# RG-LRU gates in quarters of TensorE, with the convolution's result and a half-swapped copy of it

## The chip, the cores and the metric

The kernel runs on one core of one Trainium2 chip. The metric is device time in microseconds (us) of one execution. The kernel before took 1862.1 us (median of 3 runs, 1861.45 to 1863.89).

## The reference

A two-layer trunk (D_MODEL 1024, 256 context tokens and 256 latent tokens). Each layer normalises, projects, runs three token mixers side by side, merges them, projects again, and ends with a squared-ReLU MLP. The change is inside the first mixer, the RG-LRU:

```
def rglru_coeffs(xc, a_w, a_b, x_w, x_b, lam):
    xh = xc.reshape(bn, n, LRU_BLOCKS, LRU_BLOCK_W)           # 16 blocks of 64 channels
    r = sigmoid(einsum('bnhi,hij->bnhj', xh, a_w) + a_b)      # gate r
    i = sigmoid(einsum('bnhi,hij->bnhj', xh, x_w) + x_b)      # gate i
    log_a = -8 * r * softplus(-lam)
    a = exp(log_a)
    u = sqrt(-expm1(2 * log_a)) * (i * xc)
    return a, u                                # then a linear scan h = a * h + u over the tokens
```

`xc` is a depthwise convolution (4 taps) of the projection `lx`; both directions of the scan have gate weights of their own. The output is the sum of the two directions' scans times `gelu(ly)`, where `ly` is another projection. So for each block of 64 channels four 64x64 matrices multiply the same `xc`: two gates, two directions.

## The kernel before

Activations lie with channels on the 128 partitions and the 512 tokens (context, then latent) along the free axis. A 1024x1024-type product is split in output slices of 128 channels. Each slice is one `gemm` (L216): the weight tile is loaded by SyncE's (SP's) DMA queue (`wraw`), split by ScalarE (ACT) into a rounded part `wh` (L200) and by VectorE (DVE) into the rest `wl` (L201), and then 24 matmuls of 128x512 on TensorE (PE) add up in one PSUM bank of the pool `mm` (4 banks). Three raw tiles and three split tiles are in flight, so the split of a slice waits for the product three slices earlier. Other PSUM work uses the 4 banks of the pool `mx`.

The RG-LRU stage of a layer handles 8 slices of 128 channels (two blocks each), i = 0 to 7:

- `lru_conv(i)`: a gemm of slice i of `lx` (below: **conv i**), then ACT L552 and three DVE operations L555 make `xc` of slice i.
- `lru_gates(i)` (**gate call i**): the block-diagonal 128x128 weights of slice i (`gw`, two blocks with zeros beside them) multiply `xc` in plain fp32, once for each direction and gate, four matmuls of 128x512 (L566), each into an `mx` bank. ACT empties each bank with a Tanh (L567), makes another Tanh for each direction (L571), and DVE multiplies by `xc` (L572).
- `lru_decay(i)`: two Exp on ACT (L578). For each pair of slices one Sqrt follows (L710), and then `lru_scan` of both on DVE (L585 to L595), whose result `yh` ACT rounds (L307).
- `gate_y(j)` (**branch gate j**): a gemm of slice j of `ly`, emptied by Gelu on ACT (L544). It is 128x512 in layer 0 and half as wide in layer 1, the last.

Exp, Gelu and Sqrt each need a table of functions that ACT loads (ACT_TABLE_LOAD) when it goes from one to another; Tanh is in the tables of Gelu and Exp, not in that of Sqrt. The order of the stage before, in layer 0, behind conv 0 and 1 and branch gates 0 to 2: gate call 0, conv 2, gate call 1, branch gates 3 and 4, conv 3, gate call 2, conv 4, gate call 3, branch gates 5 and 6, a small product for the next mixer, conv 5, gate call 4, conv 6, gate call 5, branch gate 7, conv 7, two gemms of the next mixer (GLA: its k and q), gate calls 6 and 7. The next mixer's first head (`gla`, its scores are the matmuls of L793) follows.

A tile scheduler orders each engine's instructions when the program is built, from program order, priorities (`tc.high_priority`) and its own estimates; on the chip each engine takes its list strictly in that order, and an instruction that waits holds back all that stand behind it.

Of the kernel before, what the change touches and what calls it, by code (L numbers as in the profile page):

```python
# [15 lines left out]
F32 = mybir.dt.float32  # L16
# [26 lines left out]
NL = 2  # L43
# [61 lines left out]
def trunk_kernel(ctx: ExitStack, tc: tile.TileContext, out: bass.AP, d: dict):  # L105
    nc = tc.nc
    V, S, G, P = nc.vector, nc.scalar, nc.gpsimd, nc.tensor
# [11 lines left out]
    sm = ctx.enter_context(tc.tile_pool(name="sm", bufs=2))  # L119
# [3 lines left out]
    def tmp():  # L123
        return t2.tile([128, 512], F32, name="t2")
# [16 lines left out]
    def mx():  # L141
        return ps_mx.tile([128, 512], F32, name="mx")
# [61 lines left out]
    def weight(*key, hi=None, lo=None, ahead=AHEAD):  # L204
        with tc.high_priority(ahead):
            return weight_parts(weight_raw(*key), hi, lo)
# [308 lines left out]
    for l in range(NL):  # L515
# [22 lines left out]
        def gate_y(i):  # L538
            if l == 0 and i < 3:
                ps = first_ps[i]  # L540
            else:
                ps = gemm(weight(l, "in", O_LY + 128 * i, hi=E_LYH), hh, hl, c0)
            ge[i] = x[:, i, :256] if last else tmp()
            S.activation(ge[i], ps, AF.Gelu_apprx_tanh)  # L544

        xcs = {}

        def lru_conv(i):
            ps = gemm(weight(l, "in", O_LX + 128 * i, hi=E_LXH, lo=E_LXL, ahead=AHEAD if l or i > 1 else 0), hh, hl, 0)
            xc = xcs[i] = tmp()  # L550

            S.activation(xc, ps, AF.Identity, scale=pc(l, "cw", 8 + i, 1), bias=pc(l, "cb", i, 1))  # L552
            x3, p3 = (a.rearrange("p (s t) -> p s t", s=2) for a in (xc, ps))
            for k, (a, b) in ((0, (1, 256)), (2, (0, 255)), (3, (0, 254))):
                V.scalar_tensor_tensor(x3[:, :, a:b], p3[:, :, a + k - 1:b + k - 1], pc(l, "cw", 8 * k + i, 1),  # L555
                                       x3[:, :, a:b], op0=ALU.mult, op1=ALU.add)

        def lru_gates(i):
            xc = xcs.pop(i)
            gw = sm.tile([128, 4, 128], F32, name="gw")  # L560
            nc.sync.dma_start(gw, d["lruw"][l, i])
            rt, tt, ix = (t[:, i % 4] for t in ws_)
            for dd in range(2):
                for q, dst in ((0, rt), (1, ix)):
                    pg = mx()
                    P.matmul(pg, gw[:, 2 * dd + q, :], xc, start=True, stop=True)  # L566
                    S.activation(dst[:, dd, :], pg, AF.Tanh, scale=0.5,  # L567
                                 bias=habx[:, l, 16 * q + 8 * dd + i:16 * q + 8 * dd + i + 1])

                c2p = c2[:, l, 1, 8 * dd + i:8 * dd + i + 1]  # L570
                S.activation(tt[:, dd, :], rt[:, dd, :], AF.Tanh, scale=c2p, bias=c2p)  # L571
                V.scalar_tensor_tensor(ix[:, dd, :], ix[:, dd, :], 1.0, xc, op0=ALU.add, op1=ALU.mult)  # L572
# [117 lines left out]
        LYS = LYS0, LYS1  # L690
        ly = iter(range(8))
# [4 lines left out]
            gate_consts()  # L696
        for i in range(0, 8, 2):
            lru_conv(i + 1)
            if i < 6:
                lru_gates(i)  # L700
                lru_conv(i + 2)
            else:

                kq0 = gla_kq(0)
                lru_gates(i)
            lru_gates(i + 1)
            for j in range(2):
                lru_decay(i + j)
            tt = ws_[1][:, i % 4:i % 4 + 2]
            S.activation(tt, tt, AF.Sqrt, scale=0.25, bias=epsc)  # L710
            for j in range(LYS[l][i // 2 + 1]):
                gate_y(next(ly))
            if i == 6:
                gates0 = gla_gates(0)
                v0 = gla_v(0)
            for j in range(2):
                lru_scan(i + j)
            if i == 6:
                ys0 = gla_r(0)
            if i == GZP:  # L720
                zs = gla_z()
# [367 lines left out]
        for c in range(5):  # L1089
            if c < 4:  # L1090
                hid[c] = ytiles(("yh", "yl")[c % 2])
                n = NSPL if c == 0 and not last else 0
# [28 lines left out]
def layout(inp):  # L1121

    import numpy as np

    f = np.float32
    A = {k: np.asarray(v) for k, v in inp.items()}
    a = {}

    def ktile(w, c, n):
        return w[:, c:c + n].reshape(8, 128, n).transpose(1, 0, 2)  # L1130

    tiles = []
    for l in range(NL):
        for w in weight_order(l):
            if w[0] == "in":
                tiles.append(ktile(A["w_in"][l], w[1], 128))
            elif w[0] == "tok":
                tiles.append(ktile(A["w_in"][l], w[1], 512)[:, 2 * w[2]:2 * w[2] + 2])
            elif w[0] == "br":
                tiles.append(ktile(A["w_branch"][l, w[1]], 128 * w[2], 128))  # L1140
            elif w[0] == "out":
                tiles.append(ktile(A["w_out"][l], 128 * w[1], 128))
            elif w[0] == "w1":
                tiles.append(ktile(A["mlp_w1"][l], 128 * w[1], 128))
            else:
                tiles.append(ktile(A["mlp_w2"][l][1024 * w[1]:1024 * w[1] + 1024], 128 * w[2], 128))
    a["wt"] = np.stack([t.reshape(128, 1024) for t in tiles])
    mw = A["mod_w"].reshape(NL, 8, 128, 12, 512)
    mw = mw[:, :, :, [0, 2, 1, 3] + list(range(4, 12))]
    mw = mw.reshape(NL, 8, 128, 6, 2, 512).transpose(0, 3, 4, 2, 1, 5).copy()  # L1150
    m0 = mw[0, :2].reshape(2, 2, 128, 8, 2, 256)
    mw[0, :2] = m0.transpose(0, 4, 2, 3, 1, 5).reshape(2, 2, 128, 8, 512)
    a["mod_w"] = mw
    xt = np.concatenate([A["ctx"][0], A["x"][0]], axis=0).T
    a["xt"] = np.ascontiguousarray(xt.reshape(8, 128, T).transpose(1, 0, 2))
    a["cs"] = np.stack([A["c_ctx"].reshape(8, 128).T, A["c"][0].reshape(8, 128).T], axis=2)
    par = np.zeros((128, NL, NPAR), f)

    def put(l, name, v):
        lo, hi = PCOLS[name]  # L1160
        par[:, l, lo:hi] = v.reshape(hi - lo, 128).T

    for l in range(NL):
        put(l, "n1", A["norm1_g"][l])
        put(l, "n2", A["norm2_g"][l])
        put(l, "modb", A["mod_b"][l])
        put(l, "cw", A["conv_w"][l])
        put(l, "cb", A["conv_b"][l])
        put(l, "ab", A["lru_a_b"][l])
        put(l, "xb", A["lru_x_b"][l])  # L1170
        put(l, "lam", A["lru_lambda"][l])
        put(l, "gb", A["gla_gate_b"][l])
        put(l, "gng", A["gla_norm_g"][l])
        put(l, "qg", A["q_norm_g"][l])
        put(l, "kg", A["k_norm_g"][l])
    a["par"] = par
    lruw = np.zeros((NL, 8, 128, 4, 128), f)
    for dd in range(2):
        for q, name in enumerate(("lru_a_w", "lru_x_w")):
            w = A[name][:, dd].reshape(NL, 8, 2, 64, 64)  # L1180
            for s in range(2):
                lruw[:, :, 64 * s:64 * s + 64, 2 * dd + q, 64 * s:64 * s + 64] = w[:, :, s]
    a["lruw"] = lruw
    glaw = np.zeros((NL, 3, 32, 2, 512), f)
    for dd in range(2):
        glaw[:, :, 16 * dd:16 * dd + 16, dd] = A["gla_gate_w"][:, None, dd]
    glaw = glaw.reshape(NL, 96, 2, 512)
    a["glaw"] = glaw
    a["wz"] = np.stack([ktile(A["w_in"][l], O_GZ, 32) for l in range(NL)])
    dim = np.arange(128)  # L1190
    swap = dim ^ 32
    rg = np.stack([A["q_norm_g"], A["q_norm_g"][:, swap], A["k_norm_g"], A["k_norm_g"][:, swap]], axis=1)
    a["ropeg"] = np.ascontiguousarray(np.broadcast_to(rg[:, None], (NL, 128, 4, 128)))
    t = np.arange(256)
    inv = (f(10000.0) ** (-np.arange(0, 64, 2, dtype=f) / f(64))).astype(f)
    ang = np.where(dim[None] < 64, (t // 64).astype(f)[:, None], (t % 64).astype(f)[:, None]) * inv[dim % 32][None]
    ang = ang.astype(f)
    sgn = np.where(dim % 64 < 32, f(-1), f(1))
    rc = np.stack([np.cos(ang), np.sin(ang) * sgn[None]]).astype(f)
    a["ropec"] = np.ascontiguousarray(rc.reshape(2, 2, 128, 128).transpose(2, 0, 1, 3))  # L1200
    a["ident"] = np.eye(128, dtype=f)
    j = np.arange(128)
    a["masks"] = np.stack([(j[:, None] <= j[None]).astype(f), (j[:, None] >= j[None]).astype(f)], axis=1)
    a["rmask"] = np.ascontiguousarray(np.broadcast_to((np.arange(T) % 64 != 0).astype(f), (128, T)))
    return {k: np.ascontiguousarray(v) for k, v in a.items()}
# [16 lines left out]
```

## Time and profile before

| | |
|---|---|
| median of 3 runs | 1862.1 us (1861.45 to 1863.89) |
| the profiled execution | 1860.73 us, span 1858.9 us, mean granted TensorE clock 0.993 |
| PE matmul busy | 1803.0 us (97%) |
| DVE busy | 1288.0 us (69%) |
| ACT busy | 936.3 us (50%) |
| gate matmuls (L566) | 128 records, 60.0 us |
| gate weights by DMA | 16 loads of 256.0 KB |

The gate matmuls appear as 128 records because one fp32 matmul is recorded as two. A record's duration includes pipeline time that overlaps its neighbours; what a matmul costs a dense stream is the distance between starts. PE is near fully busy over the whole span, but the shares of DVE and ACT differ from stage to stage: in the RG-LRU stages of both layers ACT is much busier than its 50%.

### The profile page before, as it was taken

The page shows a single profiled execution, that of the slowest core. Times are in us where ns is not written, and L with a number is a line of the kernel's source. Part 1 is how long each engine was busy: PE and PEld are TensorE (multiplying, and loading weights), DVE is VectorE, ACT ScalarE, POOL GpSimd, SP SyncE. Part 2 cuts the span into 40 slices and gives each one's busy share as a digit, 9 for nine tenths or more (in the row PEclk, how much of TensorE's full clock was granted, in tenths as well). Part 3 has the DMA queues.
Part 4 walks back from the last instruction along what each step waited for, and adds up shares of the span by engine and source line. Part 5 has one row for each costly group of instructions (what it writes and reads, how often), then busy time and mean ns, then how long its engine had stood idle before and what let it go on. Part 6 is the DMA issues. An engine that isn't in the chain of part 4 may idle for free.

```text
span 1858.9 us, 26345 instructions
## 1 busy us (share of the span) xinstructions
PE 1803.0 (97%) x9992; PEld 1496.2 (80%) x9992; DVE 1288.0 (69%) x2206; ACT 936.3 (50%) x1620; POOL 62.8 (3%) x87
## 2 busy tenths in 40 slices
PE   5999999999999999999999999999999999999999
PEld 4766788888787888988888889767889877878887
DVE  4786775454557777789763447797876588778776
ACT  4787545333444333564332325788665455556443
POOL 1000000000000000000000000000000000000000
PEclk9999999999999999999999999999999999999999
DMA  8322222232211556666753235522333432755554
GB/s 324 102 76 85 70 82 80 70 102 80 68 57 52 196 188 201 215 219 208 237 178 100 91 95 184 173 92 85 109 101 122 131 125 91 261 170 159 186 188 148
DMA packets 82143, 255.59 MB, mean 137 GB/s; under 512 B 9184, under 2 KB 12384, under 8 KB 81248
## 3 DMA queue, kind: packets, MB, share of 16 engines
q1 hardware_dynamic: 82016, 253.90, 42.0%
q8 instruction: 79, 1.29, 0.3%
q14 instruction: 48, 0.39, 0.1%
HBM read 252.82 MB, written 1.05 MB: 137 GB/s over the span
## 4 chain that ended last, share of the span: by engine, by line
PE 59%; issue 22%; DVE 9%; ACT 7%; POOL 1%; DMA 1%; SPq 0%; POOLq 0%; DVEq 0%; ACTq 0%
PE mm L216 48%; PE mx L216 5%; DVE wl L201 2%; PE mx L841 2%; ACT lru L567 1%; PE mx L220 1%; PE mx L822 1%; ACT wh L200 1%; ACT lru L710 1%; DVE lru L586 1%; PE mx L566 1%; DVE lru L588 1%; ACT lru L571 1%; PE mx L793 1%; DMA wraw<-wt 1%
## 5 line engine op out<-in xcount | busy, mean ns | idle before, releaser
L216 PE MATMUL mm<-h,wh 128*128 128x512 f32 (+1 forms) x2512 | 729.6, 370 | 7.1 <-ACT h L307 5.1
L200 ACT CAST wh<-wraw 128x1024 fp32r<-128x1024 f32 x365 | 382.2, 1049 | 500.9 <-PE mm L216 391.5
L201 DVE TENSOR_TENSOR wl<-wraw,wh 128x1024 fp32r<-128x1024 f32 x365 | 445.5, 1222 | 235.6 <-ACT wh L200 219.9
L216 PEld LDWEIGHTS mm<-h,wh 128*128 128x128 f32 x2512 | 452.4, 189 | 91.5 <-issue 7.2
L216 PE MATMUL mm<-h,wl 128*128 128x512 f32 (+1 forms) x1448 | 493.9, 341 | 0.0
L216 PEld LDWEIGHTS mm<-h,wl 128*128 128x128 f32 x1448 | 274.0, 189 | 31.6 <-issue 1.4
L216 PE MATMUL mm<-yh,wh 128*128 128x512 f32 (+1 forms) x640 | 224.7, 351 | 2.2 <-DVE big L1039 2.1
L216 PE MATMUL mm<-yh,wl 128*128 128x512 f32 (+1 forms) x640 | 224.0, 350 | 0.0
L216 PE MATMUL mm<-yl,wh 128*128 128x512 f32 (+1 forms) x640 | 222.4, 348 | 0.0
L216 PE MATMUL mm<-yp,wh 128*128 128x512 f32 (+1 forms) x576 | 183.6, 374 | 2.5 <-ACT g L873 2.3
L216 PE MATMUL mm<-wh,h 128*128 128x512 f32 x576 | 183.4, 395 | 0.0
L216 PE MATMUL mm<-yp,wl 128*128 128x256 f32 x512 | 145.1, 283 | 0.0
L370 DVE SCALAR_TENSOR_TENSOR t<-t,cs,t 128x512 f32<-128x512 f32 x178 | 127.2, 746 | 25.6 <-DMA t<-mod_w 18.7
L216 PEld LDWEIGHTS mm<-yh,wh 128*128 128x128 f32 x640 | 121.7, 190 | 17.4 <-issue 3.0
L216 PEld LDWEIGHTS mm<-yh,wl 128*128 128x128 f32 x640 | 121.2, 189 | 15.4 <-issue 0.7
L216 PEld LDWEIGHTS mm<-yl,wh 128*128 128x128 f32 x640 | 121.2, 189 | 14.9 <-issue 0.5
L216 PEld LDWEIGHTS mm<-wh,h 128*128 128x128 f32 x576 | 107.7, 188 | 23.1 <-issue 1.0
L216 PEld LDWEIGHTS mm<-yp,wh 128*128 128x128 f32 x576 | 104.1, 189 | 24.0 <-ACT g L873 2.5
L216 PE MATMUL mm<-wl,h 128*128 128x512 f32 x288 | 113.4, 394 | 0.0
L216 PEld LDWEIGHTS mm<-yp,wl 128*128 128x128 f32 x512 | 96.9, 189 | 0.8 <-issue 0.7
L216 PE MATMUL mx<-t,t 128*128 128x128 f32 (+2 forms) x416 | 81.7, 338 | 0.1
L989 ACT ACTIVATE t<-mx,mxs,rsq 128x512 f32<-128x512 f32 (+1 forms) x48 | 33.9, 709 | 74.0 <-DVE mxs L987 72.0
(223 smaller groups left out, 2006.5 us busy)
## 6 DMA issues: line engine op xcount, KB each, us to landing
wraw<-wt SPq DMA_DIRECT2D x365, 512.0 KB, 3.6
t<-mod_w SPq DMA_DIRECT2D x144, 256.0 KB, 3.5
modw<-mod_w SPq DMA_DIRECT2D x6, 2048.0 KB, 14.4
big<-xt SPq DMA_DIRECT2D x8, 512.0 KB, 5.1
gw<-lruw SPq DMA_DIRECT2D x16, 256.0 KB, 3.7
out<-big SPq DMA_DIRECT2D x8, 128.0 KB, 1.9
t<-glaw SPq DMA_DIRECT2D x8, 96.0 KB, 2.9
t<-ropeg SPq DMA_DIRECT2D x2, 256.0 KB, 3.3
```

The source lines that it names most:

```text
L200: S.copy(wh, r)
L201: (G if lo == "G" else V).tensor_tensor(wl, r, wh.bitcast(F32), op=ALU.subtract)
L216: P.matmul(o, a, b, **kw)
L220: P.transpose(o, a, ident)
L370: V.scalar_tensor_tensor(a, t, c, a, op0=ALU.mult, op1=ALU.add)
L566: P.matmul(pg, gw[:, 2 * dd + q, :], xc, start=True, stop=True)
L567: S.activation(dst[:, dd, :], pg, AF.Tanh, scale=0.5, bias=habx[:, l, 16 * q + 8 * dd + i:16 * q + 8 * dd + i + 1])
L571: S.activation(tt[:, dd, :], rt[:, dd, :], AF.Tanh, scale=c2p, bias=c2p)
L586: V.tensor_tensor(u, u, h, op=ALU.mult)
L588: V.tensor_tensor_scan(h, a, u, 0.0, op0=ALU.mult, op1=ALU.add)
L841: P.matmul(po[:, :256], a, b, start=j == 0, stop=j == len(mm) - 1)
L989: S.activation(p[:, :128 * nk], psc[:, :128 * nk], AF.Exp, scale=r, bias=mxs[:, 1:2], accum_out=mxs[:, 2:3])
```

## The change

Each gate call's four 128x512 matmuls become eight of 64x512. A 64x64 quarter of TensorE's array is addressed by the partitions of the operands (rows) and of the output (columns). The upper half of the rows now holds the weights of gate r, the lower half those of gate i; one quarter for each of the two blocks. Since both gates need both blocks, a second tile `xs` holds `xc` with its two halves of 64 partitions exchanged; two DMAs (SBUF to SBUF, on SP's queue) make it after the convolution. The zeros in `gw` go, so its load is half as large. For one direction the four quarters write two PSUM banks, a bank for each gate. The branch gates move: half of those of a pair stand between the next convolution and the first gate call, the other half between the second convolution and the second gate call; before, they stood behind the pair's Sqrt.

```
+            xs = xss[i] = gtmp()
+            nc.sync.dma_start(xs[:64], xc[64:])
+            nc.sync.dma_start(xs[64:], xc[:64])
...
-            gw = sm.tile([128, 4, 128], F32, name="gw")
+            xc, xs = xcs.pop(i), xss.pop(i)
+            gw = sm.tile([128, 2, 128], F32, name="gw")
...
             for dd in range(2):
+                pgs = mx(), mx()
+                for q in range(2):
+                    r = slice(64 * q, 64 * q + 64)
+                    for b in range(2):
+                        P.matmul(pgs[q][64 * b:64 * b + 64, :], gw[r, dd, 64 * b:64 * b + 64],
+                                 (xc if b == q else xs)[r, :], start=True, stop=True)
                 for q, dst in ((0, rt), (1, ix)):
-                    pg = mx()
-                    P.matmul(pg, gw[:, 2 * dd + q, :], xc, start=True, stop=True)
+                    pg = pgs[q]
                     S.activation(dst[:, dd, :], pg, AF.Tanh, scale=0.5,
...
             lru_conv(i + 1)
+            n = LYS[l][i // 2 + 1]
+            for j in range(0, n, 2):
+                gate_y(next(ly))
             if i < 6:
                 lru_gates(i)
                 lru_conv(i + 2)
+                for j in range(1, n, 2):
+                    gate_y(next(ly))
...
             S.activation(tt, tt, AF.Sqrt, scale=0.25, bias=epsc)
-            for j in range(LYS[l][i // 2 + 1]):
-                gate_y(next(ly))
```

In the lists of the changed program some lines have other numbers: L566 is now L575, L567 is L579, L571 is L583, L572 is L584, L578 is L590, L710 is L727, L585 is L597, L595 is L607.

On ACT in layer 0, from gate call 1 to the first pair's Sqrt (t_653 is `xc` of slice 2), before:

```order
L552 ACTIVATE t_653<-mm,par 128x512
L567 ACTIVATE lru<-mx,par 128x512 x2
L571 ACTIVATE lru<-lru,c_483 128x512
L567 ACTIVATE lru<-mx,par 128x512 x2
L571 ACTIVATE lru<-lru,c_483 128x512
L578 ACTIVATE lru<-lru,c_483 128x512 x2
L710 ACT_TABLE_LOAD
L710 ACTIVATE lru<-lru,epsc 128x2048
L200 CAST wh<-wraw 128x1024
L544 ACT_TABLE_LOAD
L544 ACTIVATE t_712<-mm 128x512
```

and now (t_735 is the Gelu of branch gate 4, t_817 is `xc` of slice 3):

```order
L544 ACT_TABLE_LOAD
L544 ACTIVATE t_735<-mm 128x512
L579 ACTIVATE lru<-mx,par 128x512 x2
L583 ACTIVATE lru<-lru,c_483 128x512
L579 ACTIVATE lru<-mx,par 128x512 x2
L583 ACTIVATE lru<-lru,c_483 128x512
L590 ACT_TABLE_LOAD
L590 ACTIVATE lru<-lru,c_483 128x512 x2
L200 CAST wh<-wraw 128x1024
L727 ACT_TABLE_LOAD
L727 ACTIVATE lru<-lru,epsc 128x2048
L552 ACTIVATE t_817<-mm,par 128x512
```

A Gelu with its table now stands ahead of gate call 1's Tanh, and the Exp behind it needs its table again. Counted over the stage, ACT's list has 16 table loads in layer 0 and 15 in layer 1, where it had 12 in each.

On DVE in layer 0, in the scans of slices 0 and 1, `xc` of slice 3 (its last two operations), before (t_800):

```order
L555 SCALAR_TENSOR_TENSOR t_800<-mm,par,t_800 128x2x255
L594 TENSOR_TENSOR lru<-lru 128x512
L555 SCALAR_TENSOR_TENSOR t_800<-mm,par,t_800 128x2x254
L595 TENSOR_TENSOR lru<-lru,t_498 128x512
L572 SCALAR_TENSOR_TENSOR lru<-lru,t_653 128x512 x2
```

and now (t_817):

```order
L606 TENSOR_TENSOR lru<-lru 128x512
L555 SCALAR_TENSOR_TENSOR t_817<-mm,par,t_817 128x2x255
L607 TENSOR_TENSOR lru<-lru,t_498 128x512
L555 SCALAR_TENSOR_TENSOR t_817<-mm,par,t_817 128x2x254
L584 SCALAR_TENSOR_TENSOR lru<-lru,t_696 128x512
```

The convolution's last operation still stands at the end of the two scans of the pair ahead of it (L595, now L607, is the last product of slice 1's scan); it moved by one operation.

On PE in layer 0, gate call 3, before:

```order
L216 MATMUL mm<-h,wh 128x512 x2
L216 MATMUL mm<-h,wl 128x512
L566 MATMUL mx<-t_800,gw 128x512 x4
L216 MATMUL mm<-h,wh 128x512 x2
L216 MATMUL mm<-h,wl 128x512
```

and now (g_822 is the exchanged copy of t_817):

```order
L216 MATMUL mm<-h,wl 128x512
L575 MATMUL mx<-t_817,gw 64x512
L216 MATMUL mm<-h,wh 128x512 x2
L216 MATMUL mm<-h,wl 128x512
L216 MATMUL mm<-h,wh 128x512 x2
L216 MATMUL mm<-h,wl 128x512
L575 MATMUL mx<-g_822,gw 64x512
L216 MATMUL mm<-h,wh 128x512 x2
L216 MATMUL mm<-h,wl 128x512
L216 MATMUL mm<-h,wh 128x512
L575 MATMUL mx<-g_822,gw 64x512
```

The call is cut: its first quarter, then six matmuls of conv 5, its second quarter, four more, and the rest. Gate call 5 and, in layer 1, calls 3 and 5 are cut in the same way; the other twelve stand whole or in groups of two and more quarters.

## Rows read from the trace of the kernel before

**Rows 1.** Stretches: length; busy PE, PEld, DVE, ACT, POOL; PEclk, DMA share, GB/s

```profile
63.15:180.50 117.35, 114.58 (x440) 81.83 (x438) 82.94 (x114) 92.66 (x118) 0.00 (x0) 0.99 0.26 83
160.00:170.00 10.00, 7.23 (x14) 2.81 (x12) 7.30 (x11) 6.42 (x11) 0.00 (x0) 0.83 0.36 132
1187.90:1291.00 103.10, 98.94 (x450) 71.61 (x449) 80.27 (x121) 90.51 (x120) 0.00 (x0) 1.00 0.29 94
```

**Rows 2.** Timeline of PE, layer 0: start, us, what, count, [idle before, releaser]

```profile
118.81 0.63 PE L216 MATMUL mm<-h,wh 128*128 128x512 f32 x2
...
124.28 3.60 PE L566 MATMUL mx<-t,gw 128*128 128x512 f32 x8
...
133.18 3.59 PE L566 MATMUL mx<-t,gw 128*128 128x512 f32 x8
...
158.41 3.60 PE L566 MATMUL mx<-t,gw 128*128 128x512 f32 x8
164.78 5.40 PE L566 MATMUL mx<-t,gw 128*128 128x512 f32 x8 [2.77 <-ACT lru L567]
```

**Rows 3.** Timeline of PE, products in tiles of 32 columns, and full fp32 ones

```profile
35.24 0.39 PE L216 MATMUL mm<-h,wl 128*128 128x512 f32 x1
35.56 1.96 PE L216 MATMUL mx<-modw,cs 128*32 128x128 f32 x64
...
220.72 1.16 PE L793 MATMUL mx<-t,t 128*128 128x128 f32 x8
```

**Rows 4.** Timeline of ACT, layer 0, first pair and gate call 2

```profile
77.37 1.52 ACT L578 ACTIVATE lru<-lru,c 128x512 f32<-128x512 f32 x2
78.90 1.28 ACT L710 ACT_TABLE_LOAD   x1
80.20 2.01 ACT L710 ACTIVATE lru<-lru,epsc 128x2048 f32<-128x2048 f32 x1
82.11 1.03 ACT L200 CAST wh<-wraw 128x1024 fp32r<-128x1024 f32 x1
...
84.45 0.60 ACT L544 ACTIVATE t<-mm 128x512 f32<-128x512 f32 x1
...
93.27 0.77 ACT L552 ACTIVATE t<-mm,par 128x512 f32<-128x512 f32 x1
93.94 1.25 ACT L567 ACTIVATE lru<-mx,par 128x512 f32<-128x512 f32 x2
...
97.77 1.28 ACT L578 ACT_TABLE_LOAD   x1
```

**Rows 5.** Timeline of DVE, layer 0, scans of slices 0 and 1

```profile
82.24 1.29 DVE L585 SCALAR_TENSOR_TENSOR lru<-lru 128x512 f32<-128x512 f32 x2 [4.54 <-ACT lru L710]
...
91.08 0.68 DVE L595 TENSOR_TENSOR lru<-lru,t 128x512 f32<-128x512 f32 x1
...
98.88 0.74 DVE L555 SCALAR_TENSOR_TENSOR t<-mm,par,t 128x508 f32<-128x508 f32 x1
```

**Rows 6.** DMA issues: what, queue, count, size, median us to landing

```profile
wraw<-wt SPq DMA_DIRECT2D x365, 512.0 KB, 3.6
...
out<-big SPq DMA_DIRECT2D x8, 128.0 KB, 1.9
```

**Rows 7.** Timeline of ACT: a rounding that waits, and each layer's last Sqrt

```profile
163.52 0.62 ACT L307 CAST yh<-lru 128x512 fp32r<-128x512 f32 x1 [3.55 <-DVE lru L595]
...
178.53 2.01 ACT L710 ACTIVATE lru<-lru,epsc 128x2048 f32<-128x2048 f32 x1
...
1288.98 2.01 ACT L710 ACTIVATE lru<-lru,epsc 128x2048 f32<-128x2048 f32 x1
```

**Rows 8.** Groups of PE, 210 to 270 us: count, busy, mean ns, idle before, releaser

```profile
L793 PE MATMUL mx<-t,t 128*128 128x128 f32 x24 | 3.5, 292 | 4.1 <-DVE t L788 4.1
```

**Rows 9.** Timeline of PE, layer 1: gate call 1, conv 3's first matmuls

```profile
1196.81 3.59 PE L566 MATMUL mx<-t,gw 128*128 128x512 f32 x8
...
1205.99 0.63 PE L216 MATMUL mm<-h,wh 128*128 128x512 f32 x2
```

More of the change, by code (lines that the diff above doesn't have):

```diff
@@ L544, in gate_y @@
             S.activation(ge[i], ps, AF.Gelu_apprx_tanh)
-        xcs = {}
+        xcs, xss = {}, {}
         def lru_conv(i):
@@ L556, in lru_conv @@
                                        x3[:, :, a:b], op0=ALU.mult, op1=ALU.add)
+            xs = xss[i] = gtmp()
+            nc.sync.dma_start(xs[:64], xc[64:])
+            nc.sync.dma_start(xs[64:], xc[:64])
         def lru_gates(i):
-            xc = xcs.pop(i)
-            gw = sm.tile([128, 4, 128], F32, name="gw")
+            xc, xs = xcs.pop(i), xss.pop(i)
+            gw = sm.tile([128, 2, 128], F32, name="gw")
             nc.sync.dma_start(gw, d["lruw"][l, i])
@@ L1176, in layout @@
     a["par"] = par
-    lruw = np.zeros((NL, 8, 128, 4, 128), f)
+    lruw = np.zeros((NL, 8, 128, 2, 128), f)
     for dd in range(2):
@@ L1181, in layout @@
             for s in range(2):
-                lruw[:, :, 64 * s:64 * s + 64, 2 * dd + q, 64 * s:64 * s + 64] = w[:, :, s]
+                lruw[:, :, 64 * q:64 * q + 64, dd, 64 * s:64 * s + 64] = w[:, :, s]
     a["lruw"] = lruw
```

## The prediction

> **What bounds the kernel now.** The table of busy times comes first: PE looks full over the whole span, so every matmul that goes seems to shorten the kernel. Second, the stretches of the two RG-LRU stages, because the change is there alone. From conv 1's end to the last Sqrt a stage takes 117.4 us in layer 0 and 103.1 us in layer 1; PE is busy 114.6 and 98.9 us of these, but ACT 92.7 and 90.5 us, DVE 82.9 and 80.3 us [rows 1]. ACT, 50% busy over the span, is 79% and 88% busy here. Third, the waits at the stage's end: gate call 7 stood 2.77 us because ACT had not emptied call 6's banks [rows 2], and ACT itself had stood 3.55 us in front of them for a scan's result on DVE [rows 7]. Fourth, what comes behind: the next mixer's scores wait 4.1 us for DVE [rows 8], and DVE's list there begins with the last pair's scans, which wait for the last Sqrt (in the first pair, 4.54 us [rows 5]). So two chains run close together: PE's dense stream, and a chain for each pair of slices: gate call, Tanh, Exp, Sqrt on ACT, scans on DVE, then the next `yh`, which holds ACT's list. The second one decides when the next mixer can start.
>
> **TensorE's part.** A gemm takes 124.28 - 118.81 = 5.47 us; from one gate call to the next with one gemm between is 8.90 us, so a call costs 3.43 us, 0.43 for each of its 8 records [rows 2]. Now a call has 16 records. If quarters never overlap it costs 6.9 us; if only two do, 3.43; if four do, 1.7. The trace has no quarter with half the rows. It has tiles of 32 columns with all rows: 64 fp32 records of 128 columns in 1.96 us, 0.03 each, where full-array records of that size take 1.16/8 = 0.14 [rows 3]; with the tail that a duration includes, that is close to four abreast. I take four abreast, as the nearest row. Ahead of those tiles PE started 0.32 us after the last matmul's start instead of the dense 0.23 (5.47/24) [rows 3]; I allow 0.2 for entering and leaving: 1.9 us a call. Four calls are cut: two quarters run alone (0.86 each), the rest takes 1.7, each entry its 0.2 or so: 4.0 us. PE's work falls by 12 x 1.5 - 4 x 0.6 = 16 us.
>
> The Trainium skill, TensorEngine Tiling (Array Packing), section Tiling Modes, says that tiles run independently and that changing the mode drains the engine; the 0.32 us fits the drain, and no run here shows two row halves at once. Its section Performance Considerations warns of the opposite end: tiling speeds up TensorE and not the emptying of PSUM. By that rule alone calls 6 and 7, which stand side by side, would give nothing, 3 us less than the 16; the 2.77 us wait at call 7 agrees, and the walk below finds more than that.
>
> **ACT's part.** Seven more table loads (4 and 3), each 1.30 us from start to start [rows 4]: 5.2 us in layer 0, 3.9 in layer 1, on an engine with 25 and 13 us free. The branch gates come earlier, so a pair's Sqrt has more gemms ahead of it, while the convolution two slices on still waits in DVE's list behind the whole scan of that pair. To see what that does I walk layer 0 along the lists, with durations from rows 4 (Tanh work of a call 97.77 - 93.94 = 3.8; two Exp 1.5; Sqrt 1.9; rounding of a weight 1.0; `xc` 0.7; Gelu 0.6).
>
> - Conv 1 ends at 63.2 (the left edge in rows 1). Branch gate 3, call 0, conv 2, branch gate 4: 3 x 5.45 + 1.9, so 81.4.
> - ACT then: weight 1.0, load 1.3, Gelu 0.6, call 1's Tanh 3.8, load 1.3, Exp 1.5, weight 1.0, load 1.3, Sqrt 1.9: 13.7, the first Sqrt ends at 95. Before it ended at 82.1 [rows 4].
> - DVE: conv 3's `xc` was finished 98.88 + 0.74 - 82.24 = 17.4 us behind the scans' start [rows 5]; now, with one `wl` fewer and one product more, about 17: 112.
> - PE reaches call 3 after call 1, conv 3, branch gate 5, call 2, conv 4, branch gate 6: 81.4 + 2 x 1.9 + 4 x 5.45 = 107. It stands 5 us for `xc`. The exchanged copy lands later by a DMA of 2 x 128 KB: between 1.9 us (128 KB) and 3.6 (512 KB) [rows 6], I take 2.5; six matmuls (1.4) cover part of it: 1 us more. Before, no such wait stood there: `xc` was ready at 99.6 [rows 5].
> - From call 3's first result (115.5) to the second Sqrt's end: 3.8 + 1.5 + two loads + 1.9: 126. `yh` of slice 2 stops ACT until the scan, 9.5 us from first operation to L595's end [rows 5]: 135.5. Behind it ACT has the rest of call 4, the small product's copies and conv 5's `xc`: 140.5; DVE finishes that at about 145. PE reached call 5 at 141: 4 us, and 0.5 for the copy.
> - Call 5 is through at about 152, k and q of the next mixer (7/8 of conv 7 is done by then) end at 162, call 6 follows, against 158.4 before [rows 2]. The third Sqrt ends at 160, its scans let ACT go on at 171 in the middle of call 6's Tanh; calls 6 and 7, four Exp, a second `yh`, two weights, one load and Sqrt: 183. Before: 178.53 + 2.0 = 180.5 [rows 7]. Layer 0 loses 2.5 us.
>
> In layer 1 a branch gate takes only (1205.99 - 1196.81 - 3.43)/2 = 2.9 us [rows 9], so PE has 2.5 us less to do for each of five and ACT's chain is as long. The same walk from 1187.9 gives Sqrts that end at 1217, 1245, 1278 and 1299.5, the last against 1291.0 [rows 7]; PE stands 5.5 us at call 3 and 4 us at call 5. Layer 1 loses 8.5 us.
>
> The clock: behind the 2.77 us wait call 7 took 5.40 us against 3.60, and the stretch around it was granted 0.83, between the levels of 1.2 and 2.4 GHz [rows 1, 2]. Four waits of 4 to 5.5 us are new. If each costs as much, 1.8 x 4 = 7 us; if it hides in the next wait, nothing; I take 2.
>
> What costs nothing: the half-size `gw`, and SP's 32 new issues. Behind a copy that waits for `xc`, SP's list has weight tiles whose raw buffer comes free later than that `xc` (three raw and three split tiles deep), so PE does not see it. Without that cover a weight would come late by up to 3.6 us [rows 6] at two places in a layer.
>
> **Sum.** 1860.7 (the profiled execution) + 2.5 + 8.5 + 2 = 1873.7. That execution lay 1.4 us under the median of 1862.1, so a median of 1875 goes with it; I say 1874. The walk's steps are sure to some 3 us in a layer.
>
> **Rivals.**
> 1. *PE stays the bound, faster.* If ACT and DVE keep up (the waits shown at calls 3 and 5 don't come about, because `xc` is ready when PE is), the whole 16 us show: 1862 - 16 = 1846. For it: PE is busy 98% and 96% of the stages [rows 1]. Against: ACT alone needs 92.7 + 5.2 and 90.5 + 3.9 us, so layer 1 can't gain more than 8.7, and its list waits for DVE.
> 2. *Waits half as long as walked*: each layer's saving and loss cancel, 1862 with 4 to either side.
> 3. *Quarters don't overlap across the row halves.* Two abreast: 3.43 + 0.2 a call, no saving, and each chain longer by 1.7 us for its calls; some 20 us slower, 1881. One at a time: 16 x 3.4 = 55 more on PE, some 1920. For it: no row shows it otherwise.
>
> **How the numbers follow.** Late `xc` and the added loads: 0.62, 1864 to 1886 by itself. Rival 1: 0.17. Rival 2: 0.13. Rival 3: 0.08, most of it two abreast. A difference under 0.2%, 3.7 us, can't be told from none. Faster: rival 1 and a little of 2, 0.20. The same: the rest of 2 and the forecast's low edge, 0.14. Slower: 0.66. The range 1857 to 1890 leaves out rival 1's middle and quarters one at a time.
>
> **What would show it.** Right: gate calls of 2 us or so where they stand whole; PE waiting at calls 3 and 5 for DVE's L555 or a copy; Sqrts ending later by 10 us and more in the middle of the stages; seven more table loads. Wrong: calls of 3.4 us or longer (rival 3), or last Sqrts that end before 180.5 and 1291.0 (rival 1).

## The result and the profile after

The changed kernel takes 1875.8 us (median of 4 runs, 1872.73 to 1877.95) against 1861.78 us (1859.26 to 1863.89): ratio 1.0075, 95% interval 1.0053 to 1.0096. The profiled execution is the slowest but one, 1877.8 us with a span of 1876.0, which is 17.1 us above the span of before.

Stretches of the changed kernel, columns as in [rows 1]: the two stages, each from conv 1's end to the last Sqrt, then three pieces of layer 0 around gate call 3.

```profile
62.60:187.00 124.40, 115.00 (x507) 76.39 (x506) 84.08 (x114) 98.36 (x121) 0.00 (x0) 0.95 0.31 89
1194.20:1306.30 112.10, 102.94 (x525) 68.39 (x524) 80.59 (x121) 94.84 (x123) 0.00 (x0) 0.97 0.35 103
...
100.00:107.30 7.30, 7.30 (x33) 5.74 (x31) 7.30 (x12) 6.46 (x10) 0.00 (x0) 1.00 0.19 72
107.30:111.90 4.60, 0.04 (x1) 0.01 (x1) 4.60 (x8) 1.47 (x4) 0.00 (x0) 0.77 0.23 86
111.90:116.60 4.70, 4.68 (x8) 2.10 (x8) 4.63 (x7) 2.75 (x3) 0.00 (x0) 0.50 0.52 105
```

The stages grew from 117.35 and 103.10 us [rows 1] to 124.40 and 112.10: 7 and 9 us, nearly all of the loss. ACT's busy time grew by 5.7 and 4.3 us, close to the seven added table loads (5.2 and 3.9).

PE in layer 0: gate call 0 with its neighbours, then call 3.

```profile
68.01 0.39 PE L216 MATMUL mm<-h,wl 128*128 128x512 f32 x1
68.33 0.64 PE L575 MATMUL mx<-t,gw 64*64 64x512 f32 x1
...
70.20 0.73 PE L216 MATMUL mm<-h,wh 128*128 128x512 f32 x2
...
106.95 0.39 PE L216 MATMUL mm<-h,wl 128*128 128x512 f32 x1
111.92 1.94 PE L575 MATMUL mx<-t,gw 64*64 64x512 f32 x2 [4.58 <-ACT yh L307]
113.79 1.22 PE L216 MATMUL mm<-h,wh 128*128 128x512 f32 x2
...
116.64 1.07 PE L575 MATMUL mx<-g,gw 64*64 64x512 f32 x2
...
118.76 0.64 PE L575 MATMUL mx<-g,gw 64*64 64x512 f32 x1
```

A whole call costs 70.20 - 68.33 = 1.87 us, so four quarters do run abreast. The first of them starts 0.32 us after the last matmul of the gemm ahead. Call 3 waits 4.58 us; two records behind the wait take 1.94 us, at half clock (granted 0.50 above). The releaser named, a rounding on ACT, is not an operand. `xc` of slice 3 is the one, ready at 111.81, as DVE's rows show:

```profile
110.49 0.68 DVE L607 TENSOR_TENSOR lru<-lru,t 128x512 f32<-128x512 f32 x1
111.08 0.73 DVE L555 SCALAR_TENSOR_TENSOR t<-mm,par,t 128x508 f32<-128x508 f32 x1
```

The first quarter that reads the copy (`mx<-g`) runs at 116.64, and ACT can empty the first bank only after that one. PE does not stand for the copy there: the six matmuls of conv 5 that its list has in between take 2.85 us at half clock, from 113.79 to 116.64. ACT's first Tanh of call 3, and the Sqrts that answer to [rows 4, 7]:

```profile
92.95 2.01 ACT L727 ACTIVATE lru<-lru,epsc 128x2048 f32<-128x2048 f32 x1
...
117.75 0.69 ACT L579 ACTIVATE lru<-mx,par 128x512 f32<-128x512 f32 x1 [3.08 <-PE mx L575]
...
126.71 2.01 ACT L727 ACTIVATE lru<-lru,epsc 128x2048 f32<-128x2048 f32 x1
...
160.53 2.01 ACT L727 ACTIVATE lru<-lru,epsc 128x2048 f32<-128x2048 f32 x1
...
185.16 2.01 ACT L727 ACTIVATE lru<-lru,epsc 128x2048 f32<-128x2048 f32 x1
...
1304.27 2.01 ACT L727 ACTIVATE lru<-lru,epsc 128x2048 f32<-128x2048 f32 x1
```

They end at 95.0, 128.7, 162.5 and 187.2; 95, 126, 160 and 183 were forecast. The time is as forecast. Whether its causes are the ones forecast was open: the forecast laid the loss on the new places of the branch gates, with 1 us for each late copy.

### The profile page after: what moved, and what is told of

Its sections match the earlier page's. It is cut to its first block, busy times and chain, and to the rows that moved or that the text cites. A ratio compares the mean times of both kernels' runs of the same rounds, so it can differ in the third digit from the quotient of the medians.

```text
span 1876.0 us, 26683 instructions
## 1 busy us (share of the span) xinstructions
PE 1805.0 (96%) x10120; PEld 1486.4 (79%) x10120; DVE 1288.7 (69%) x2206; ACT 946.8 (50%) x1627; POOL 67.2 (4%) x87
## 4 chain that ended last, share of the span: by engine, by line
PE 28%; issue 20%; DVE 5%; ACT 3%; DMA 1%; POOL 1%; POOLq 0%; SPq 0%; DVEq 0%; ACTq 0%
PE mm L216 23%; PE mx L216 2%; DVE wl L201 1%; ACT wh L200 1%; PE mx L856 1%; PE mx L837 1%; DMA wraw<-wt 1%; DMA g<-t 0%; PE mx L220 0%; PE mx L575 0%; DVE t L555 0%; ACT lru L727 0%; POOL t L439 0%; ACT lru L579 0%; DVE lru L598 0%
```

## The experiments

Ratios are to the kernel before on the same chip, with 95% intervals; 0.1% is 1.9 us.

| label | places of the branch gates | gates | copy | ratio |
|---|---|---|---|---|
| (changed) | new | quarters | DMA | 1.0075 (1.0053 to 1.0096) |
| e1_places | new | whole | none needed | 1.0030 (1.0014 to 1.0045) |
| e2_quarters | old | quarters | DMA | 1.0073 (1.0050 to 1.0096) |
| e3_nocopy | new | quarters | none | 1.0007 (0.9989 to 1.0025) |
| e10_unread | new | quarters | DMA, not read | 1.0009 (0.9996 to 1.0022) |
| e8_old_nocopy | old | quarters | none | 1.0012 (1.0003 to 1.0021) |
| e9_old_pool | old | quarters | GpSimd | 1.0087 (1.0072 to 1.0102) |
| e13_new_pool | new | quarters | GpSimd | 1.0091 (1.0069 to 1.0112) |
| e4_gelutanh | new, no Gelu table | quarters | DMA | 1.0053 (1.0038 to 1.0068) |
| e5_convfirst | new, conv first | quarters | DMA | 1.0048 (1.0033 to 1.0063) |
| e12_pool_convfirst | new, conv first | quarters | GpSimd | 1.0023 (1.0011 to 1.0035) |
| e11_nocopy_convfirst | new, conv first | quarters | none | 1.0012 (0.9994 to 1.0030) |
| e14_before_convfirst | old, conv first | whole | none needed | 1.0010 (0.9996 to 1.0023) |

**The new places alone.** Into the kernel before, the two loops over `gate_y` of the change in place of the one behind the Sqrt; the gates stay whole:

```
             lru_conv(i + 1)
+            n = LYS[l][i // 2 + 1]
+            for j in range(0, n, 2):
+                gate_y(next(ly))
             if i < 6:
                 lru_gates(i)
                 lru_conv(i + 2)
+                for j in range(1, n, 2):
+                    gate_y(next(ly))
...
             S.activation(tt, tt, AF.Sqrt, scale=0.25, bias=epsc)
-            for j in range(LYS[l][i // 2 + 1]):
-                gate_y(next(ly))
```

> The gates of before (four full-array matmuls, no copy), the branch gates in the new places. ACT's list is then that of the changed kernel but for a few neighbours, with the same 15 table loads in a layer. Theory (late xc in ACT's and DVE's lists decides): calls 0 to 2 cost PE 4.6 us more, so the first Sqrt ends near 98 instead of 95 and PE reaches call 3 at 112; xc comes at about 115, the wait is some 3 us instead of 4.6, and call 3 runs through in 3.4 us without a copy. Time 1870 us, 1864 to 1876: most of the loss stays. Rival A (the quarters with their copy are the loss, by half-clock and DMA latency): 1858 to 1864. Rival B (the places alone are the loss and quarters give or take nothing): 1873 to 1879.

1868.2 us (1863.93 to 1869.77), inside the theory's range. Its steps were less good: the first Sqrt ended at 95.6, not 98, `xc` of slice 3 came at 112.4, not 115, and the wait was 1.85 us, not 3. With whole gates the places cost some 6 us, not all of the loss.

**The quarters alone.** In the changed kernel the two loops over `gate_y` go, and the branch gates stand behind the Sqrt again:

```
...
             S.activation(tt, tt, AF.Sqrt, scale=0.25, bias=epsc)
+            for j in range(LYS[l][i // 2 + 1]):
+                gate_y(next(ly))
```

> Quarters and copy, the branch gates behind the Sqrt as before. Table loads 12 and 13. Theory: the first Sqrt comes as early as before (82), xc of slice 3 at about 100 and PE reaches call 3 no earlier than that, so there is no wait at call 3; PE's 1.5 us a call shows until ACT is full (25 us free in layer 0, 13 in layer 1), half of the 16: 1854 us, 1848 to 1862. Rival A (quarters with their copy are the loss): 1866 to 1880. Rival B (places alone): 1854 too, since then nothing else speaks against the quarters; it differs from the theory in e1.

1876.9 us (1872.51 to 1878.57), as slow as the whole change. This contradicts the theory, which expected 1854.

**Without the copy.** 

```
-            xs = xss[i] = gtmp()
-            nc.sync.dma_start(xs[:64], xc[64:])
-            nc.sync.dma_start(xs[64:], xc[:64])
+            xss[i] = xc
```

> The changed kernel without the exchanged copy: the quarters that need it read xc as it stands, so half of the gate sums use the wrong block, and the two DMAs of each slice go. Theory: PE still waits for xc at calls 3 and 5, some 4.5 and 3 us in layer 0; only what the copy adds behind xc goes, 1 to 2 us at each of four places: 1871 us, 1866 to 1875. Rival A (the copy's latency is the loss): 1858 to 1864.

1861.6 us (1857.51 to 1867.26): the whole loss is gone, where 1 to 2 us a place were expected. PE's wait at call 3 is not gone, nor the half clock behind it (PE at call 3 of this run; then two of its stretches, the one behind the wait and layer 1's stage):

```profile
111.28 3.69 PE L573 MATMUL mx<-t,gw 64*64 64x512 f32 x16 [4.59 <-ACT yh L307]
...
111.20:115.90 4.70, 4.62 (x19) 1.42 (x20) 4.67 (x7) 4.67 (x7) 0.00 (x0) 0.52 0.18 45
...
1188.00:1292.20 104.20, 96.95 (x524) 67.97 (x523) 80.39 (x123) 94.72 (x123) 0.00 (x0) 0.97 0.30 90
```

What changed is what follows `xc`. In layer 1, call 5 of the changed kernel (timeline of all engines):

```profile
1270.33 0.74 DVE L555 SCALAR_TENSOR_TENSOR t<-mm,par,t 128x508 f32<-128x508 f32 x1
...
1271.33 1.04 PE L575 MATMUL mx<-t,gw 64*64 64x512 f32 x2 [1.76 <-DVE t L555]
...
1275.16 1.07 PE L575 MATMUL mx<-g,gw 64*64 64x512 f32 x2 [0.99 <-DMA g<-t]
...
1276.27 0.69 ACT L579 ACTIVATE lru<-mx,par 128x512 f32<-128x512 f32 x1 [5.42 <-PE mx L575]
```

and of this run without a copy:

```profile
1260.66 0.74 DVE L555 SCALAR_TENSOR_TENSOR t<-mm,par,t 128x508 f32<-128x508 f32 x1
...
1261.65 1.95 PE L573 MATMUL mx<-t,gw 64*64 64x512 f32 x16 [1.52 <-DVE t L555]
...
1262.77 0.69 ACT L577 ACTIVATE lru<-mx,par 128x512 f32<-128x512 f32 x1 [2.68 <-PE mx L573]
```

From the last convolution operation's end to ACT's first Tanh it is 5.2 us with the copy and 1.4 without. PE shows a wait of only 0.99 us for the copy, because it did seven matmuls meanwhile; ACT shows 5.42. ACT is the one that matters. One thing is not kept equal in this pair: without the copy the scheduler also orders ACT's, DVE's and PE's lists differently.

**The copies made, but not read.**

```
-                                 (xc if b == q else xs)[r, :], start=True, stop=True)
+                                 xc[r, :], start=True, stop=True)
```

> The changed kernel with both copies made by DMA as they are, but no quarter reads them (half of the gate sums use the wrong block). The lists of ACT and DVE are those of the kernel without copies. If the wait for the copy is the loss: 1862 us, 1858 to 1865, as without copies. If SP's list, which waits for xc in front of weights, or the transfers themselves are the loss: 1868 to 1876.

1861.5 us (1858.14 to 1866.54): the transfers and SP's issues cost nothing that can be measured. What costs is that the quarters read the copy, together with the order of the lists that the scheduler makes for it: ACT's, DVE's and PE's lists here are those of the run without a copy. The next pair keeps them nearly equal.

**Quarters in the old places, without a copy and with one by GpSimd.** The first is e2_quarters with `xss[i] = xc`; the second with

```
+            G.tensor_copy(xs[:64], xc[64:])
+            G.tensor_copy(xs[64:], xc[:64])
```

> Quarters, branch gates behind the Sqrt as before, and no exchanged copy: the quarters that need it read xc as it stands (half of the gate sums use the wrong block). ACT's list is that of before but for two places. Revised theory (the copy's latency in front of ACT's first Tanh is the loss; the places cost 6.7 us and the quarters give back 6.6 where no copy is waited for): 1855 us, 1850 to 1859. Theory of the prediction (PE's saving is worth nothing once ACT's and DVE's chain decides): 1860 to 1863.

> Quarters, branch gates behind the Sqrt as before, and the exchanged copy made by two GpSimd copies of 64x512 instead of two DMAs; everything is computed. The engines' lists are those of the kernel without a copy. A GpSimd product of 128x512 took 1.29 us before, so an estimate of 1.2 to 2.6 us for both copies where the DMAs land 2.2 us after their issue of 0.5 each. Revised theory (latency of the copy, and the cut calls that it brings): 1858 us, 1853 to 1863. If it is any wait for a second operand, however short: 1866 to 1876.

1862.4 us (1858.65 to 1865.71) and 1876.8 us (1873.62 to 1878.63). Between the two, ACT's, DVE's and SP's lists are the same instruction for instruction, PE's but for two matmuls at layer 1's last gate call. So 0.75%, 14 us, is the price of GpSimd's copy and the wait for it. The loss needs neither a DMA nor the cut calls, which the revised theory had blamed: GpSimd's copy has neither and costs as much. And without a copy the quarters bring nothing in the old places; 1855 had been expected. Timeline of layer 0's call 7 without a copy, then of layer 1's Sqrts and the last convolution operation of slices 3, 5 and 7:

```profile
163.33 4.40 PE L573 MATMUL mx<-t,gw 64*64 64x512 f32 x16 [7.15 <-ACT lru L577]
...
1206.06 2.01 ACT L720 ACTIVATE lru<-lru,epsc 128x2048 f32<-128x2048 f32 x1
...
1221.57 0.72 DVE L555 SCALAR_TENSOR_TENSOR t<-mm,par,t 128x508 f32<-128x508 f32 x1
...
1232.09 2.01 ACT L720 ACTIVATE lru<-lru,epsc 128x2048 f32<-128x2048 f32 x1
...
1249.98 0.74 DVE L555 SCALAR_TENSOR_TENSOR t<-mm,par,t 128x508 f32<-128x508 f32 x1
...
1261.62 2.01 ACT L720 ACTIVATE lru<-lru,epsc 128x2048 f32<-128x2048 f32 x1
...
1278.27 0.72 DVE L555 SCALAR_TENSOR_TENSOR t<-mm,par,t 128x508 f32<-128x508 f32 x1
...
1290.58 2.01 ACT L720 ACTIVATE lru<-lru,epsc 128x2048 f32<-128x2048 f32 x1
```

and layer 1's with GpSimd's copy:

```profile
1210.06 2.01 ACT L722 ACTIVATE lru<-lru,epsc 128x2048 f32<-128x2048 f32 x1
...
1225.57 0.72 DVE L555 SCALAR_TENSOR_TENSOR t<-mm,par,t 128x508 f32<-128x508 f32 x1
...
1239.45 2.00 ACT L722 ACTIVATE lru<-lru,epsc 128x2048 f32<-128x2048 f32 x1
...
1257.34 0.74 DVE L555 SCALAR_TENSOR_TENSOR t<-mm,par,t 128x508 f32<-128x508 f32 x1
...
1270.77 2.01 ACT L722 ACTIVATE lru<-lru,epsc 128x2048 f32<-128x2048 f32 x1
...
1287.41 0.72 DVE L555 SCALAR_TENSOR_TENSOR t<-mm,par,t 128x508 f32<-128x508 f32 x1
...
1304.52 2.01 ACT L722 ACTIVATE lru<-lru,epsc 128x2048 f32<-128x2048 f32 x1
```

Without a copy PE comes early to call 7 and stands 7.15 us for ACT's emptying, where it stood 2.77 [rows 2]; it also stands 2.14 us at call 3 and 1.53 at call 5 for `xc`, where it did not wait before. Two thirds of the 12 us that eight calls save in layer 0 (1.5 each) turned into these waits.

From one Sqrt to the next layer 1 takes 26.0, 29.5 and 29.0 us without the copy, 29.4, 31.3 and 33.8 with it: each pair pays again, 3.4, 1.8 and 4.8 us. That is a loop. A pair's Sqrt releases its scans; in DVE's list the last convolution operations of the next odd slice stand among them; that slice's gate call, Tanh, Exp and the next Sqrt follow. From a Sqrt to the next `xc` the two runs take the same, to 0.01 us (15.51, 17.89 and 16.65 from start to start); all that is added lies between `xc` and the next Sqrt. So in these turns it is not that GpSimd's copies slow DVE's scans. In layer 1 the copy is paid once a turn. In layer 0 the first turn alone pays: the Sqrts stand 2.7 and 0.4 us further apart, then 1.0 us closer.

**GpSimd's copy in the new places.** The same edit in the changed kernel; its lists are those of e3_nocopy.

> New places, quarters and the exchanged copy made by GpSimd; all lists but GpSimd's are those of the run in the new places without a copy (1861.6 us). Theory (the wait for the copy on the chain of a pair, 2 to 4.5 us where GpSimd copies beside DVE's scans, at calls 3 and 5 of a layer and once more in layer 1): 1874 us, 1868 to 1879. If the new places leave room for a copy where the old ones didn't: 1862 to 1867.

1878.6 us (1874.47 to 1882.4), 0.84% over its twin without a copy, whose lists are the same on ACT, DVE, PE and SP. The two prices, 0.75% and 0.84%, are not told apart: the places do not change them.

**Without Gelu's table.** `AF.Gelu_apprx_tanh` of the branch gates becomes `AF.Tanh`:

> The changed kernel with Tanh in place of the branch gates' Gelu, so that ACT's table stays: 7 loads in a layer's stage instead of 15, 10 us less on ACT. Theory: the first Sqrt ends some 2.6 to 4 us earlier (91 to 92), xc of slice 3 by as much, the wait at call 3 falls to 1 us or nothing, and all chains of pairs shorten: 1861 us, 1854 to 1868. If table loads don't matter (PE or DVE alone sets the end): 1873 to 1878.

1872.6 us (1868.38 to 1875.43). The first Sqrt ends at 89.4 instead of 95.0, but eight or nine fewer loads in a layer give only 0.22%, and the intervals overlap. Both expectations missed, the second by 0.4 us; the loads are at most a small part.

**The convolution first.** ACT's and DVE's operations of `lru_conv` are put under a high priority, so that `xc` of slice 3 no longer waits for the first pair's scans:

```
+            with tc.high_priority(1000):
+                S.activation(xc, ps, AF.Identity, ...)
...
+            with tc.high_priority(1000):
+                for k, (a, b) in ((0, (1, 256)), (2, (0, 255)), (3, (0, 254))):
+                    V.scalar_tensor_tensor(x3[:, :, a:b], ...)
```

In the changed kernel, then without a copy, then with GpSimd's copy:

> The changed kernel with the convolution's ACT and DVE operations at a high priority: the last operations of xc of slice 3 stand ahead of the first pair's scans instead of in them, slice 5's still among those of the second pair. Prediction's theory (late xc): PE reaches call 3 with xc and copy ready, so the wait of 4.6 us and the half clock behind it go in layer 0 and as much in layer 1, while scans come 2.3 us later: 1866 us, 1860 to 1871. If only the copy's latency counts, wherever xc is: 1873 to 1878.

> New places, quarters that all read xc (half of the gate sums use the wrong block), and the convolution's ACT and DVE operations at a high priority. Conv first gave back 6.6 us where the copy is waited for. If late xc costs by itself: 1855 us, 1850 to 1859, the wait of 4.6 us at call 3 gone. If conv first only helped by hiding the copy: 1860 to 1864, as without it.

> The same with the exchanged copy made by GpSimd and read, everything computed; ACT's, DVE's, PE's and SP's lists are those of the run without a copy, instruction for instruction. If the copy costs only where PE or ACT stands for it (calls 3, 5 and 7, where xc is late): call 3 no longer stands for it, call 5 still does: 1862 us, 1857 to 1867. If GpSimd's copies cost wherever they run: as much above the run without a copy as in the old places, 14 us: 1868 to 1876.

1869.2 us (1867.98 to 1870.34), 1865.7 (1857.5 to 1870.23) and 1865.9 (1861.15 to 1868.59). `xc` of slice 3 is now ready at 94 and PE reaches call 3 at 106 without a wait. GpSimd's copy costs 0.11% against its twin (1.0023 and 1.0012, the intervals overlap) where it cost 0.75% and 0.84%. GpSimd's copies do lengthen DVE's work, by some 4 us over the two stages here (from 83.43 and 79.67 us busy to 85.17 and 82.44) and by 2.2 in the run before with GpSimd's copy in the new places; the run with more of it is the one without a price that can be told. So GpSimd's copy costs where `xc` comes late. And late `xc` alone costs nothing that can be told: without a copy, conv first gains nothing (1.0012 against 1.0007, each to 0.18%). The DMA copy keeps 0.36% more than none. Layer 1's call 0 in the run with the DMA copy shows one place:

```profile
1194.09 0.50 SPq L562 DMA_DIRECT2D g<-t  x1
...
1194.36 1.07 PE L577 MATMUL mx<-t,gw 64*64 64x512 f32 x2
1198.58 1.07 PE L577 MATMUL mx<-g,gw 64*64 64x512 f32 x2
```

The copy is issued at 1194.09 behind other transfers in SP's list, and the first quarter that reads it starts 4.2 us after the call's first quarter. From slice 0's `xc` to layer 1's first Sqrt it is 31.8 us, 27.3 in the run without a copy; to the last Sqrt 109.9 and 103.1. So in these two profiles 4.6 of layer 1's 6.9 us are there by the first Sqrt. Their lists differ too, so the split of the 0.36% is not shown.

**The convolution first in the kernel before.** The same two lines, nothing else:

> The kernel before with the convolution's ACT and DVE operations at a high priority and nothing else. Before, PE stood for late xc 0.83 us at layer 1's call 3 and 2.64 us at its call 7, nowhere in layer 0. xc comes earlier there, the scans behind it up to 2.3 us later: 1862 us, 1857 to 1866. If the late xc of calls 3 and 7 were what holds layer 1: 1854 to 1858.

1863.2 us (1859.53 to 1867.75), no difference. No version here beats the kernel before; quarters with a copy come closest in e12_pool_convfirst.

## Why the prediction held in time and failed in a term

- **TensorE's part, right.** 1.9 us a call was forecast from tiles with all rows; 1.87 was measured. Rival 3 is out. What this is worth is nearly nothing: 0.23% in the new places (e3_nocopy against e1_places, whose intervals overlap), none in the old (e8_old_nocopy). Rival 1 falls with that: not even without a copy, and in the old places, does PE's time show. The forecast also weighed a rule of the Trainium skill, TensorEngine Tiling (Array Packing), section Performance Considerations: tiling does not speed up the emptying of PSUM. The 7.15 us wait for ACT at call 7 agrees; the waits for `xc` at calls 3 and 5 are not of that kind.
- **The walk in layer 0, right up to call 3.** Gate call 1 at 81.31 (81.4 forecast), first Sqrt 95.0 (95), PE at call 3 at 107.3 (107), `xc` at 111.8 (112), wait 4.58 us (5).
- **The copy, wrong.** The failed step is "six matmuls (1.4) cover part of it: 1 us more". It priced the copy at PE, which has other work to fill in. At call 3 PE does not wait for the copy at all; the six matmuls, at half clock, took 2.85 us and stood between `xc` and the quarter that ACT needed. The copy is paid by ACT: both quarters of a bank must be there before its Tanh, so the delay from `xc` to the first Tanh counts whole, 5.9 us instead of 2.7 at layer 0's call 3 and 5.2 instead of 1.4 at layer 1's call 5. It is paid on a loop, at several pairs. The term was some 1 us at each of four places; the runs give 11 to 16 us in all (0.61% in the old places and 0.68% in the new by DMA, 0.75% and 0.84% by GpSimd). The figures by DMA hold also what the scheduler's other order of the lists costs.
- **The places and the loads, mis-sized the other way.** The forecast drew its whole loss from the branch gates' places and the added loads. With whole gates the places cost 0.30%, with quarters nothing (e2_quarters against the change, e8_old_nocopy against e3_nocopy); why whole gates pay for them is not shown. The wait for late `xc` that the walk found is real, but it stays in e3_nocopy, 4.59 us at call 3, and that is as fast as before. The two errors cancelled in the sum, so that the time came out is luck.
- **The sum.** 2.5 + 8.5 + 2 us were forecast, 13 over the profiled execution; 7 and 9 us in the stages and 1 outside were seen. Layer 0's stage took 124.4 us for 119.8 walked (183 - 63.2). Without the copy it takes 121.6 (e3_nocopy, 61.9 to 183.5), so the copy cost 2.8 us there where 1.5 were forecast, and the walk itself was 3.3 us short; that part is not traced. In layer 1 PE's waits were smaller than walked (1.15 and 1.76 us at calls 3 and 5 for 5.5 and 4) and the copy larger: without it the stage takes 104.20 us, 1.1 above before. To add up the ends of the last Sqrts was itself unsafe: the 121.6 us of e3_nocopy are 4.25 more than before, and that kernel is no slower.
- **SP's issues, half right.** Unread copies cost nothing. But in layer 1 the second half of slice 0's copy is issued at 1197.10 behind other transfers, 2.9 us after the first, and call 0 goes on at 1202.42 only; the forecast had no copy that lands late there:

```profile
1194.21 0.50 SPq L560 DMA_DIRECT2D g<-t  x1
...
1197.10 0.50 SPq L561 DMA_DIRECT2D g<-t  x1
...
1202.42 0.61 PE L575 MATMUL mx<-g,gw 64*64 64x512 f32 x1 [0.58 <-DMA g<-t]
```

- **The clock, not borne out.** Half clock behind call 3's wait is shown (0.50 over 4.7 us). But e3_nocopy has the same wait and 0.52 over 4.7 us behind it, its profiled execution has the same mean granted clock as the changed kernel's (0.988), and it is as fast as before. So of the forecast's 2 us nothing shows by itself. What half clock adds where it lengthens the way from `xc` to the Tanh, as with the six matmuls at call 3, no run separates.

## What to carry to other kernels

An engine that is 97% busy over a span need not be what a stage waits for: nearly halving the gate calls' time there turned into longer waits for their operand and for the engine that empties PSUM. In these runs a copy in front of an operand is priced at the consumer that ends last, and again at each turn where the operand lies on a loop; look for what releases the operand before pricing its transfer, and take the operand off the end of the loop first (the convolution first, with GpSimd's copy, was the cheapest of the versions with a copy). A forecast whose time comes out is not yet a forecast whose causes are right: undoing each part alone is what separated them.

## What the hardware showed unexpectedly

Four 64x64 quarters, two of each row half, run abreast: 16 fp32 records of 512 columns in 1.87 us, 0.12 us each, where a full-array record takes 0.43. Of the 32 GpSimd copies of 64x512 in e9_old_pool 27 took 0.61 to 1.02 us; the others took up to 2.72, beside DVE's products, as at layer 0's call 3:

```profile
98.72 2.72 POOL L560 COPY g<-t 64x512 f32<-64x512 f32 x1 [20.93 <-DVE t L555]
99.08 1.29 DVE L584 SCALAR_TENSOR_TENSOR lru<-lru,t 128x512 f32<-128x512 f32 x2
...
100.28 0.68 DVE L308 TENSOR_TENSOR yl<-lru,yh 128x512 fp32r<-128x512 f32 x1
...
101.49 1.22 DVE L201 TENSOR_TENSOR wl<-wraw,wh 128x1024 fp32r<-128x1024 f32 x1 [0.53 <-ACT wh L200]
101.50 1.69 POOL L561 COPY g<-t 64x512 f32<-64x512 f32 x1
...
108.27 0.92 POOL L560 COPY g<-t 64x512 f32<-64x512 f32 x1 [5.08 <-DVE t L555]
...
109.25 0.61 POOL L561 COPY g<-t 64x512 f32<-64x512 f32 x1
```

The Trainium skill, SBUF — State Buffer, section SBUF: two separate sides, says that DVE and GpSimd share a pair of ports, which one instruction holds for its whole length: a GpSimd operation, or one of DVE with two SBUF inputs, as those shown. The rows agree: the first copy ends at 101.44, 0.5 us behind the last of DVE's three operations, and the second at 103.19, 0.5 us behind the next one. No run here isolates it.
